# Tree attention on one core: ScalarE copies K out of PSUM, the transposes lead PE's iteration, GpSimd spreads a part of V

## The chip, the cores and the metric

One core of a Trainium2 chip. PE is its matrix engine; in this kernel PE's results stand in a memory called PSUM, and VectorE or ScalarE copies them to SBUF, the memory that the next steps read. The metric is the device time of one execution in microseconds, median of several; lower is better. The kernel before runs at 159.24 us (three runs, 158.61 to 160.22). Line numbers such as L263 in profile lines are those of each kernel's own file, so the same statement has another number in another kernel.

## The reference

Attention in which query i sees only itself and its ancestors in a binary tree over the sequence. Eight batches, twelve heads, 512 positions, 64 dimensions, float32.

```python
mask[i, i] = 1
parent = i
while parent > 0:
    parent = (parent - 1) // 2
    mask[i, parent] = 1
scores = np.einsum('bhqd,bhkd->bhqk', Q, K) * scale
scores = scores + (1 - mask) * (-1e9)
weights = np.exp(scores - np.max(scores, axis=-1, keepdims=True))
weights = weights / (np.sum(weights, axis=-1, keepdims=True) + 1e-10)
return np.einsum('bhqk,bhkd->bhqd', weights, V).astype(np.float32)
```

## The kernel before

The work is cut into 48 pairs of heads, six pairs a batch. Each pair goes through three steps: `transposes` (PE turns Q and K into PSUM, VectorE copies both to SBUF), `scores` (PE multiplies, ScalarE takes three exponentials), `values` (PE multiplies the weights with V, VectorE normalises, the result is stored). Besides, VectorE spreads V into a layout that the sparse products need ("V copies", two halves a batch, nine copies each). GpSimd issues the loads, which cast float32 to bf16 on the way.

```python
def load(b):                       # six stage buffers per tensor
    ...
    elif b < B - 1:
        plan = ((V, 0, H), (Q, 0, 6), (K, 0, 6), (Q, 6, H), (K, 6, H))
    else:
        plan = ((V, 0, H), (Q, 0, 6), (K, 0, 6), (Q, 6, 10), (K, 6, 10),
                (Q, 10, H), (K, 10, H))
    ...                            # one nc.gpsimd.dma_start per entry

def transposes(i):
    b, hp = pairs[i]
    if hp == 0:
        load(b)
    tp = psumT.tile([P, 2, 512], bf16)     # Q in [:, 0, :], K in [:, 1, :]
    ...                                    # 16 transposes on PE
    qk = work.tile([P, 2, 512], bf16)
    nc.vector.tensor_copy(out=qk[:, :, :], in_=tp[:, :, :])

# the loop; the order of PE, VectorE and ScalarE is the order of the program
for i in range(N):
    b, hp = pairs[i]
    if i + 1 < N:
        scores(i + 1)
    if i + 2 < N:
        transposes(i + 2)
    values(i)
    ...                                    # V copies of this or the next batch on VectorE
```

The softmax here doesn't subtract the row's maximum and nothing guards it: scores larger than these inputs give would overflow.

Of the kernel before, what the change touches and what calls it, by code (L numbers as in the profile page):

```python
# [123 lines left out]
def kernel(  # L124
# [7 lines left out]
    nc = tc.nc  # L132
    B, H, S, D = Q.shape
    P = nc.NUM_PARTITIONS
    assert (S, D) == (512, 64) and H % 2 == 0
    T = 4
    HP = H // 2
# [52 lines left out]
    def load(b):  # L190
        qs = stage.tile([P, H, T * D], bf16)
        ks = stage.tile([P, H, T * D], bf16)
        vs = stage.tile([P, H, T * D], bf16)
        if b == 0:
            plan = ((Q, 0, 2), (K, 0, 2), (V, 0, 6), (Q, 2, 6), (K, 2, 6),
                    (V, 6, H), (Q, 6, H), (K, 6, H))
# [5 lines that stand above are left out]
        for src, h0, h1 in plan:  # L202
            dst = qs if src is Q else ks if src is K else vs
            nc.gpsimd.dma_start(  # L204
                out=dst[:, h0:h1, :],
                in_=src[b, h0:h1].rearrange("h (p t) d -> p h (t d)", t=T),
            )
        loaded[b] = (qs, ks, vs)

    def spread(b, half):  # L210
        vs = loaded[b][2]
        v1, vx = v1s[b % NV], vxs[b % NV]
        n = H // 2
        h0, h1 = n * half, n * half + n
        v = vs[:, h0:h1, :].rearrange("p h (t d) -> p h t d", t=T)
        ops = [(vx[64:P, h0:h1, :, 0:D], v[64:P, :, :, :])]
        for par in range(2):
            slots = slice(0, 4, 3) if par else slice(1, 3)
            for a in range(2):
                ops.append((  # L220
                    vx[32 * a:32 * a + 32, h0:h1, slots, 0:D],
                    v[32:64, :, 2 * a + par, :].unsqueeze(2).to_broadcast(
                        [32, n, 2, D]
                    ),
                ))
        for r in range(T):
            ops.append((
                v1[32 * r:32 * r + 32, h0:h1, 0:D], v[0:32, :, ORD[r], :]
            ))
        return ops  # L230

    def copies(ops):
        for o, i in ops:
            nc.vector.tensor_copy(out=o, in_=i)  # L234
# [3 lines left out]

    def transposes(i):
        b, hp = pairs[i]  # L240
        if hp == 0:
            load(b)
        qs, ks, vs = loaded[b]
        tp = psumT.tile([P, 2, 512], bf16)

        for sel, src, order in ((0, qs, ident), (1, ks, permk)):
            for t in range(T):
                for hi in range(2):
                    o = tp[D * hi:D * hi + D, sel, :]
                    if sel == 0:  # L250
                        o = o[:, P * t:P * t + P]
                    else:
                        lo = 64 * ORD[t]
                        step = 256 + 64 * t - lo
                        o = o[:, lo:].rearrange(
                            "d (c x) -> d c x", x=64
                        )[:, 0:step // 64 + 1:step // 64, :]
                    nc.tensor.matmul(  # L258
                        out=o, lhsT=src[:, 2 * hp + hi, D * t:D * t + D],
                        rhs=order, start=True, stop=True, is_transpose=True,  # L260
                    )
        qk = work.tile([P, 2, 512], bf16)
        nc.vector.tensor_copy(out=qk[:, :, :], in_=tp[:, :, :])  # L263
        state[i] = qk

    def scores(i):
# [57 lines left out]
    def values(i):  # L324
        b, hp = pairs[i]
        v1, vx = v1s[b % NV], vxs[b % NV]
        et1, etx, ete = state.pop(i)
        o2 = psumO.tile([P, 2, 512], fp32)
        for hi in range(2):
            h = 2 * hp + hi  # L330
            for t in range(T):
                w = [(et1[:, hi, P * t:P * t + P], v1[:, h, 0:D + 1]),
                     (etx[:, hi, t, :], vx[:, h, t, 0:D + 1])]
                if t < 2:
                    w.append((ete[:, hi, 96 * t:96 * t + P],
                              vx[:, h, 1 - t, 0:D + 1]))
                for n, (e, v) in enumerate(w):
                    nc.tensor.matmul(  # L338
                        out=o2[:, hi, (D + 1) * t:(D + 1) * (t + 1)],
                        lhsT=e, rhs=v, start=n == 0, stop=n == len(w) - 1,  # L340
                    )
        o4 = o2[:, :, 0:T * (D + 1)].rearrange("p h (t x) -> p h t x", t=T)
        rec = opool.tile([P, 2, T, 1], fp32)
        nc.vector.reciprocal(out=rec[:, :, :, :], in_=o4[:, :, :, D:D + 1])  # L344
        of = opool.tile([P, 2, T * D], fp32)
        nc.vector.tensor_tensor(  # L346
            out=of[:, :, :].rearrange("p h (t d) -> p h t d", t=T),
            in0=o4[:, :, :, 0:D],
            in1=rec[:, :, :, :].to_broadcast([P, 2, T, D]),
            op=ALU.mult,  # L350
        )
        nc.sync.dma_start(
            out=out[b, 2 * hp:2 * hp + 2].rearrange(
                "h (p t) d -> p h (t d)", t=T
            ),
            in_=of[:, :, :],
        )

    N = len(pairs)
    E = mybir.EngineType  # L360
    with tc.manual_schedule(engines={E.PE, E.DVE, E.Activation}):
        transposes(0)
        scores(0)
        transposes(1)
        copies(spread(0, 0))
        todo = []
        for i in range(N):
            b, hp = pairs[i]
            if i + 1 < N:
                scores(i + 1)  # L370
            if i + 2 < N:
                transposes(i + 2)
            values(i)
            if hp == 0:
                todo = spread(b, 1)
            elif hp == HP - 2 and b + 1 < B:
                todo = spread(b + 1, 0)
            if hp in (0, 1, 2):
                lo, hi = ((0,) + (3, 6, 9))[hp:hp + 2]
                copies(todo[lo:hi])  # L380
            elif hp >= HP - 2 and b + 1 < B:
                copies(todo[0:4] if hp == HP - 2 else todo[4:9])


# [28 lines left out]
```

## Time and profile before

| | before |
|---|---|
| time, median | 159.24 us |
| profiled span | 158.6 us, granted PE clock 0.989 |
| busy PE / VectorE / ScalarE / GpSimd | 78 / 79 / 58 / 24 % |
| last load packet | 140.5 us |
| first to last normalising multiply | 19.91 to 154.47 us, 2.86 us a pair |

The prediction below shows the page's engine shares and slices. Read them as an average over a long middle, in which both VectorE and the DMA queues are full, and a last part after about 140 us in which only the engines work. Two more lines, from the page's chain of what ended last and from the view of waits, will be needed for comparison:

```profile
DMA 65%; DVE 19%; PE 6%; POOL 5%; issue 3%; POOLq 0%
```

```profile
ACT et L291 <- PE st L273: 60.0, 48, 6.7
```

The chain goes through loads for 65% of the span. ScalarE waited 60.0 us in total, 48 times (once a pair), and always for PE's scores.

### The profile page before, as it was taken

To read this page: it belongs to the slowest core of one execution; us is meant where nothing else is said; L and a number is where in the kernel's file an instruction comes from. 1 tells how busy PE (TensorE), PEld (TensorE's weight loads), DVE (VectorE), ACT (ScalarE), POOL (GpSimd) and SP (SyncE) were. 2 spreads that over 40 slices of the span, in tenths; PEclk is the share of its full clock that TensorE was granted. 3 is DMA by queue.
4 is the path that set the end of the run, shared out by engine and by line. 5 is a ranking of instruction groups with operands and counts; after the bars stand their busy time and mean duration, and the time that the engine had idled before them with its cause. 6 is when DMAs were issued, how large, how long until landed. Compare 5 with 4: busy or idle time off the path is not lost.

```text
span 158.6 us, 6339 instructions
## 1 busy us (share of the span) xinstructions
PE 123.9 (78%) x2784; PEld 82.8 (52%) x2784; DVE 125.0 (79%) x300; ACT 92.3 (58%) x145; POOL 38.2 (24%) x49
## 2 busy tenths in 40 slices
PE   0437698987889589968978789968998787968960
PEld 0213566654556357746655565745665654645640
DVE  4104889699988999799959999799969995799951
ACT  3041357665667458766674676855866668546840
POOL 7955412322242222420224222240321000000000
PEclk9999999999999999999999999999999999999995
DMA  5999999999999999999999999999999999622432
GB/s 117 145 174 197 201 195 221 235 231 227 227 232 227 238 222 223 245 228 229 225 228 239 220 223 238 225 243 221 223 244 221 231 233 237 179 81 72 133 107 94
DMA packets 50811, 32.23 MB, mean 203 GB/s; under 512 B 1504, under 2 KB 50656, under 8 KB 50784
## 3 DMA queue, kind: packets, MB, share of 16 engines
q0 software_dynamic: 37584, 18.88, 87.9%
q1 hardware_dynamic: 13200, 12.96, 28.8%
q8 instruction: 21, 0.34, 0.8%
q14 instruction: 6, 0.05, 0.1%
HBM read 38.13 MB, written 12.58 MB: 320 GB/s over the span
## 4 chain that ended last, share of the span: by engine, by line
DMA 65%; DVE 19%; PE 6%; POOL 5%; issue 3%; POOLq 0%
DMA ks<-in_K_dram 53%; DMA qs<-in_Q_dram 12%; DVE of L346 6%; DVE vx L234 6%; DVE qk L263 3%; PE o L338 3%; DVE v L234 3%; POOL vs L204 2%; DVE rec L344 2%; POOL qs L204 2%; POOL ks L204 1%; PE tp L258 1%; PE stx L273 1%; PE st L273 1%; POOLq L397 0%
## 5 line engine op out<-in xcount | busy, mean ns | idle before, releaser
L291 ACT ACTIVATE et<-st 128x1024 bf16<-128x1024 f32 x48 | 49.1, 1023 | 60.0 <-PE st L273 60.0
L263 DVE COPY qk<-tp 128x1024 bf16<-128x1024 bf16 x48 | 32.9, 685 | 20.0 <-PE tp L258 19.3
L338 PE MATMUL o<-v,et 128*128 128x65 bf16 x384 | 36.5, 195 | 10.2 <-DVE v L234 9.1
L273 PEld LDWEIGHTS <-qk 64*64 64x64 bf16 (+1 forms) x864 | 19.9, 108 | 36.9 <-issue 20.1
L312 ACT ACTIVATE etx<-stx 128x768 bf16<-128x768 f32 x48 | 38.7, 805 | 0.0
L338 PEld LDWEIGHTS <-et 128*128 128x128 bf16 x384 | 30.7, 98 | 14.5 <-DVE v L234 10.3
L338 PE MATMUL o<-vx,etx 128*128 128x65 bf16 x384 | 36.1, 194 | 0.0
L346 DVE TENSOR_TENSOR of<-o,rec 128x512 f32<-128x512 f32 x48 | 33.2, 692 | 1.7
L234 DVE COPY vx<-vs 32x768 bf16<-32x768 bf16 (+1 forms) x80 | 33.0, 412 | 1.6
L338 PEld LDWEIGHTS <-etx 128*128 128x128 bf16 x384 | 31.4, 98 | 1.2 <-issue 1.2
L338 PE MATMUL o<-vx,ete 128*128 128x65 bf16 x192 | 27.7, 195 | 0.0
L258 PE MATMUL tp<-ctile,qs 128*64 128x128 bf16 x384 | 20.9, 232 | 8.3 <-DMA qs<-in_Q_dram 8.3
L273 PE MATMUL st<-qk 64*128 64x512 bf16 x96 | 19.2, 396 | 8.5 <-DVE qk L263 8.1
L204 POOL DMA_DIRECT2D qs<-in_Q_dram x18 | 14.9, 826 | 43.8 <-DMA vs<-in_V_dram 29.9
L258 PE MATMUL tp<-ctile,ks 128*64 128x128 bf16 x384 | 19.6, 226 | 2.9 <-DMA ks<-in_K_dram 2.9
L204 POOL DMA_DIRECT2D ks<-in_K_dram x18 | 14.6, 809 | 26.4 <-DMA qs<-in_Q_dram 13.6
L273 PE MATMUL st<-ctile 64*128 64x512 bf16 x96 | 19.7, 400 | 0.3 <-issue 0.3
L273 PE MATMUL stx<-qk 64*64 64x64 bf16 (+2 forms) x768 | 19.9, 211 | 0.0
L338 PEld LDWEIGHTS <-ete 128*128 128x128 bf16 x192 | 18.4, 98 | 0.0
L234 DVE COPY v<-vs 32x384 bf16<-32x384 bf16 x64 | 17.6, 275 | 1.0
L258 PEld LDWEIGHTS <-qs 128*64 128x64 bf16 x384 | 12.8, 113 | 9.7 <-DMA qs<-in_Q_dram 8.4
L273 PE MATMUL stx<-ctile 64*128 64x448 bf16 x96 | 17.6, 363 | 0.0
(14 smaller groups left out, 59.2 us busy)
## 6 DMA issues: line engine op xcount, KB each, us to landing
out_dram<-of SPq DMA_DIRECT2D x48, 256.0 KB, 6.3
qs<-in_Q_dram POOLq DMA_DIRECT2D x14, 384.0 KB, 25.9
ks<-in_K_dram POOLq DMA_DIRECT2D x14, 384.0 KB, 26.1
vs<-in_V_dram POOLq DMA_DIRECT2D x7, 768.0 KB, 28.0
vs<-in_V_dram POOLq DMA_DIRECT2D x2, 384.0 KB, 8.9
qs<-in_Q_dram POOLq DMA_DIRECT2D x2, 256.0 KB, 17.1
ks<-in_K_dram POOLq DMA_DIRECT2D x2, 256.0 KB, 17.0
ctile<-tree_consts SPq DMA_DIRECT2D x1, 368.0 KB, 3.0
```

The lines of the kernel that those rows point to most:

```text
L204: nc.gpsimd.dma_start(out=dst[:, h0:h1, :], in_=src[b, h0:h1].rearrange("h (p t) d -> p h (t d)", t=T),)
L234: nc.vector.tensor_copy(out=o, in_=i)
L258: nc.tensor.matmul(out=o, lhsT=src[:, 2 * hp + hi, D * t:D * t + D], rhs=order, start=True, stop=True, is_transpose=True,)
L263: nc.vector.tensor_copy(out=qk[:, :, :], in_=tp[:, :, :])
L273: nc.tensor.matmul(out=dst, lhsT=lhsT, rhs=rhs, start=first, stop=True, skip_group_check=not first,)
L291: nc.scalar.activation(out=et1[:, :, :], in_=st1[:, :, :], func=AF.Exp, scale=scale)
L312: nc.scalar.activation(out=etx[:, :, :, 32:P], in_=stx[:, :, 0:384].rearrange("p h (c q) -> p h c q", c=T), func=AF.Exp, scale=scale,)
L338: nc.tensor.matmul(out=o2[:, hi, (D + 1) * t:(D + 1) * (t + 1)], lhsT=e, rhs=v, start=n == 0, stop=n == len(w) - 1,)
L344: nc.vector.reciprocal(out=rec[:, :, :, :], in_=o4[:, :, :, D:D + 1])
L346: nc.vector.tensor_tensor(out=of[:, :, :].rearrange("p h (t d) -> p h t d", t=T), in0=o4[:, :, :, 0:D], in1=rec[:, :, :, :].to_broadcast([ ...
```

## The change

The intent is to take work off VectorE. ScalarE copies the K half of each transposed tile, GpSimd takes three of the nine V copies of each half, and PE does the transposes of pair i+2 ahead of the scores of pair i+1, so that the copies have longer. As GpSimd's order is now fixed by the program, loads are issued one batch ahead by hand.

```diff
-        ops = [(vx[64:P, h0:h1, :, 0:D], v[64:P, :, :, :])]
+        ops = []
 ...
-        return ops
+        ops.insert(0, (vx[64:P, h0:h1, :, 0:D], v[64:P, :, :, :]))
+        for o, i in ops[0:3]:
+            nc.gpsimd.tensor_copy(out=o, in_=i)
+        return ops[3:]
 ...
-        if hp == 0:
-            load(b)
+        if hp == 0 and b + 1 < B:
+            load(b + 1)
 ...
-        nc.vector.tensor_copy(out=qk[:, :, :], in_=tp[:, :, :])
+        nc.vector.tensor_copy(out=qk[:, 0, :], in_=tp[:, 0, :])
+        nc.scalar.copy(out=qk[:, 1, :], in_=tp[:, 1, :])
 ...
-    with tc.manual_schedule(engines={E.PE, E.DVE, E.Activation}):
+    with tc.manual_schedule(engines={E.PE, E.DVE, E.Activation, E.Pool}):
+        load(0)
 ...
+            if i + 2 < N:
+                transposes(i + 2)
             if i + 1 < N:
                 scores(i + 1)
-            if i + 2 < N:
-                transposes(i + 2)
             values(i)
 ...                                  # the V copies left to VectorE shared out anew: 2, 2, 2 and 3, 3
```

More of the change, by code (lines that the diff above doesn't have):

```diff
@@ L378 @@
             if hp in (0, 1, 2):
-                lo, hi = ((0,) + (3, 6, 9))[hp:hp + 2]
+                lo, hi = (0, 2, 4, 6)[hp:hp + 2]
                 copies(todo[lo:hi])
             elif hp >= HP - 2 and b + 1 < B:
-                copies(todo[0:4] if hp == HP - 2 else todo[4:9])
+                copies(todo[0:3] if hp == HP - 2 else todo[3:6])
 _INS = ['Q', 'K', 'V']
```

## The prediction

> **What bounds the kernel now.** I read the whole-run page first (engine shares, the 40 slices, the queue lines), then GpSimd's own timeline, the timeline around one stall, and the groups. The page:
>
> ```profile
> PE 123.9 (78%) x2784; PEld 82.8 (52%) x2784; DVE 125.0 (79%) x300; ACT 92.3 (58%) x145; POOL 38.2 (24%) x49
> ...
> DVE  4104889699988999799959999799969995799951
> ACT  3041357665667458766674676855866668546840
> ...
> DMA  5999999999999999999999999999999999622432
> ...
> q0 software_dynamic: 37584, 18.88, 87.9%
> q1 hardware_dynamic: 13200, 12.96, 28.8%
> ```
>
> Two things look full: VectorE (nine tenths in most slices) and the 16 DMA engines (nine tenths from slice 2 to slice 34, that is to about 139 us; then six tenths and less). VectorE invites the reading "the kernel is VectorE bound, so take work off it", which is the intent of the change. GpSimd's timeline says which of the two leads. GpSimd keeps eight loads in flight, so each issue is released by the landing of the load eight places before it. The V issues of a batch are released by the landing of the first K chunk of the batch two before; the last batch is split more finely, and there a Q issue is released by that of batch 6:
>
> ```profile
> 46.54 1.01 POOL L204 DMA_DIRECT2D vs<-in_V_dram  x1 [1.68 <-DMA ks<-in_K_dram]
> ...
> 63.90 1.01 POOL L204 DMA_DIRECT2D vs<-in_V_dram  x1 [2.37 <-DMA ks<-in_K_dram]
> ...
> 83.05 1.01 POOL L204 DMA_DIRECT2D vs<-in_V_dram  x1 [2.17 <-DMA ks<-in_K_dram]
> ...
> 100.43 1.01 POOL L204 DMA_DIRECT2D vs<-in_V_dram  x1 [2.54 <-DMA ks<-in_K_dram]
> ...
> 117.06 0.70 POOL L204 DMA_DIRECT2D qs<-in_Q_dram  x1 [1.92 <-DMA ks<-in_K_dram]
> ```
>
> So the first K chunk of batches 2 to 6 landed at about 46.5, 63.9, 82.6 (the chain of waits has it ending there), 100.4 and 117.0, and the timeline below shows that of batch 7 at 135.0: (135.0 - 46.5)/5 = 17.7 us a batch. VectorE's multiply that normalises a pair ("of") starts at 55.83 for the first pair of batch 2 and 72.82 for batch 3, where no load is waited for: 17.0 us a batch. The two are within 4%, and the loads are the slower. The packets agree: 37584/8 + 13200/8 = 6348 packets a batch, and in the middle of the run each engine finishes one every 43.8 ns (2920 packets per 8 us on 16 engines, counted in the trace), so 6348 x 43.8/16 = 17.4 us.
>
> The stall at the last batch, then VectorE in the rows of the groups:
>
> ```profile
> 134.70 0.28 ACT L317 ACTIVATE ete<-stx 128x128 bf16<-128x128 f32 x1
> ...
> 135.04 0.41 PE L258 MATMUL tp<-ctile,ks 128*64 128x128 bf16 x8 [1.11 <-DMA ks<-in_K_dram]
> 135.50 0.69 DVE L263 COPY qk<-tp 128x1024 bf16<-128x1024 bf16 x1 [2.08 <-PE tp L258]
> ```
>
> The reader is to see that at 135.0 all engines had run dry and PE started again on a landing. Eight pairs (40 to 47) are still to be normalised; their multiplies start at 136.45 ... 154.47, and the span ends at 158.6. The end is therefore: landing of the last batch's first K chunk (135.0) plus a tail of 23.6 us. Only the tail can be shortened by faster engines; 135.0 is set by the queues.
>
> **What the Trainium skill says.** (1) "SBUF — State Buffer", Who interferes with whom: VectorE in a two-port mode and GpSimd hold a shared port pair exclusively, the other waits. The trace agrees: the 384-element V copy has a median of 251 ns, and this one, started inside a GpSimd issue, took 0.62 us and ended with it:
>
> ```profile
> 24.50 0.82 POOL L204 DMA_DIRECT2D qs<-in_Q_dram  x1 [4.22 <-DMA vs<-in_V_dram]
> ```
> ```profile
> 24.75 0.62 DVE L234 COPY v<-vs 32x384 bf16<-32x384 bf16 x1
> ```
>
> (2) "GPSIMD Engine Reference", 4.1 Engine selection: an operation with one input runs at roughly line rate; its section 3.1 gives 1.03 cycles an element for short bodies and 2.6 for two inputs. No row of this trace has a GpSimd copy. (3) "ScalarE: Activation LUTs", What ACT_TABLE_LOAD costs: 186 ns + 0.833 ns an element, neighbours overlapping by 93 ns. Agrees: 1024, 768 and 128 elements took 1023, 805 and 284 ns, and the busy total 92.3/48 = 1.92 us a pair is less than their sum, 2.11, by two overlaps of 0.09. (4) "VectorE: DVE Perf Modes", Why PSUM operands drop a tier: at most two elements a cycle from PSUM; the 1024-element copy at 685 ns (533 + about 150) fits.
>
> **The change part by part.** Rows used:
>
> ```profile
> L291 ACT ACTIVATE et<-st 128x1024 bf16<-128x1024 f32 x48 | 49.1, 1023 | 60.0 <-PE st L273 60.0
> L263 DVE COPY qk<-tp 128x1024 bf16<-128x1024 bf16 x48 | 32.9, 685 | 20.0 <-PE tp L258 19.3
> ...
> L346 DVE TENSOR_TENSOR of<-o,rec 128x512 f32<-128x512 f32 x48 | 33.2, 692 | 1.7
> ...
> L234 DVE COPY vx<-vs 32x768 bf16<-32x768 bf16 x64 | 23.7, 371 | 1.1
> L234 DVE COPY v<-vs 32x384 bf16<-32x384 bf16 x64 | 17.6, 275 | 1.0
> ```
>
> VectorE a pair before: 0.685 + 0.692 + 0.20 (reciprocal) + V copies 50.5/48 = 1.05, sum 2.63, plus gaps of some 0.2: the 2.83 us of 17.0/6. After: the Q half of the copy is 512 elements, about 0.42 (267 + 150 ns); a batch keeps 4 + 8 of its 18 V copies, 4 x 0.371 + 8 x 0.275 = 3.7 us or 0.61 a pair. Sum 0.42 + 0.69 + 0.20 + 0.61 = 1.92, with gaps 2.1. It frees 0.7 us a pair.
>
> ScalarE gains a 512-element copy, about 0.60 us by the slope between its rows ((1023 - 284)/896 = 0.825 ns an element), 0.51 where it overlaps: 1.92 + 0.51 to 0.60 = 2.4 to 2.5 us a pair. It becomes the fullest engine beside PE, whose tightest pair before took 2.35 us (63.78 to 66.13). I expect 2.5 us a pair where nothing else waits.
>
> PE's order: transposes first gives the copies of Q and K a whole iteration before the scores need them, which takes away PE's waits for qk (8.1 us at matmuls, mostly hidden now). It costs something at a stall: a late K chunk now holds back the scores of the pair before, which before were already done.
>
> GpSimd gains per batch 2 copies of 1536 and 4 of 768 elements. At one element a cycle of 1.2 GHz and 0.2 us each (an estimate from the GPSIMD page): 2 x 1.5 + 4 x 0.84 = 6.4 us, beside five issues of about 0.85. The built order shows five loads of the next batch, then the six copies, with no load issued between. So issuing pauses 6.4 us a batch. With eight loads in flight and one landing every 3.5 us, five or more stay queued: the DMA engines stay full. The first copies wait until the fifth issue of batch 1, at about 14.3; the first half is spread at about 17.5, and the first value products before began at 18.4. No loss.
>
> So until the last K chunk nothing moves: 17.4 to 17.7 us a batch from the queues, engines able to do 15. T stays 135.0. The tail from T: K transposes 0.45; scores and first exponential of pair 41 to T+2.0; its remaining exponentials to T+2.95; five more pairs at 2.5 bring pair 46 to T+15.5; pair 47 without a copy in front, +1.9 = T+17.4; value products 0.75, reciprocal 0.25, so the last multiply starts at T+18.4, against 154.47 - 135.04 = T+19.4 before. The rest (multiply, store, 4.1 us) is unchanged. Gain 1.0 us: 159.24 - 1.0 = 158.2.
>
> **The rivals.** (A) VectorE leads, not the queues: then 17.0 us a batch becomes 15, eight batches save 16 us, about 143. For it: VectorE's slices at 9. Against it: the landings 17.7 us apart with full DMA slices, and PE waiting for K at five places; 7.5 batches of queue work cannot shrink. I give it 5%, even in a small form (155). (B) GpSimd's copies are slow. At 2.6 cycles an element the six take 13.5 us; with issues 17.7, just the pace of the queues; above that GpSimd sets the pace and every 1 us costs 8. (C) The lock: VectorE's two-port copies (350 ns for 768 elements is four a cycle) wait for whole GpSimd copies. Those of a batch start about when its first Q chunk lands, and VectorE's own copies of that batch start some 5 us later, so short GpSimd copies collide with two or three, 1 to 2 us a batch inside a slack of 5; slow ones could collide with seven and cost more than the slack. B and C together would give 162 to 175. (D) ScalarE at 2.7 rather than 2.5 us a pair: still under 2.9, the queues' pace, but the tail is then 1.4 us longer: 159.5.
>
> **Range and chances.** Centre 158.2. Low 156.0: the tail at PE's 2.35 a pair saves 1.9, and T may come 1 us earlier. High 161.5: D, with a late V spread in batch 6, whose GpSimd copies stand behind the finer-split last loads (issued till 120.7) and could hold PE 1 to 3 us if slow. Faster by over 2% (below 156.05) 0.10; within 0.76; slower (above 162.4) 0.14.
>
> **What would show it.** Right: DMA slices still 9 to about slice 34, first K chunks landing 17 to 18 us apart and the last at 134 to 136; VectorE's busy time near 95 us and ScalarE's near 118; a GpSimd copy of 1536 elements at 1.3 to 1.7 us; PE idle mostly put down to loads; the last eight multiplies 2.5 us apart. Wrong: DMA slices below 9 in the middle with K chunks further apart (B), V copies on VectorE far above 371 ns (C), or K chunks landing earlier (A: the queues were held back by something I did not see).

## The result, and the profile after

The changed kernel takes 182.97 us (four runs, 182.8 to 187.37) against 159.05 for before with one more run: a ratio of 1.149, 95% interval 1.141 to 1.157. Ratios here are the mean time of one kernel's fast runs over that of the other's fast runs of the same rounds, so they are not quite the ratio of the medians quoted. Executions over 1.5% slower than the fastest of the same kernel are left out of the means. The profiled execution of the changed kernel was its slowest (187.37 us).

The page of the changed kernel, engine shares, slices and chain:

```profile
PE 132.5 (72%) x2784; PEld 93.1 (50%) x2784; DVE 112.3 (61%) x252; ACT 114.6 (62%) x193; POOL 87.6 (47%) x97
...
DVE  3019778487465947495684775585844685457511
ACT  2321456874855568847568776729578867796750
...
DMA  6999999999999999999999999996131322133122
...
DMA 25%; PE 21%; DVE 18%; ACT 18%; issue 10%; POOL 5%; ACTq 0%; POOLq 0%
```

No engine is full any more, and the DMA engines are no longer full after slice 27 (about 125 us; the last load packet ended at 129.4, before at 140.5). The chain no longer hangs on one thing: DMA 25% where it was 65%, and PE, VectorE and ScalarE share the rest. That is the picture of engines that wait for one another in turn. From the first to the last normalising multiply the kernel now takes 22.02 to 180.78 us, 3.38 us a pair instead of 2.86: 47 x 0.515 = 24.2 us, with the 2.1 us later start all of the 26.3 us between the two spans.

The loads did not end early because they were faster. The queues share the engines between loads and stores: when the last load packet ended, 8143 of 13056 store packets had been moved, before 11135. With the pairs slower, fewer stores competed.

The waits of the changed kernel (total us, times, longest):

```profile
ACT qk L267 <- DVE qk L266: 62.2, 32, 6.5
...
DVE rec L348 <- PE o L342: 52.8, 40, 2.9
PE st L277 <- ACT et L295: 26.4, 20, 3.3
```

ScalarE's idle time is as long as before (62.2 against 60.0), but it stands elsewhere: not before the exponential for PE, but before the new K copy, for VectorE's Q copy. VectorE in turn waits for PE's value products and PE for ScalarE's exponentials. The timeline of the changed kernel, at a point where no loads and no GpSimd copies are left, shows the loop once (start us, duration, engine, instruction; in brackets the idle time before it and what ended it):

```profile
148.42 0.30 ACT L321 ACTIVATE ete<-stx 128x128 bf16<-128x128 f32 x1
...
148.63 0.38 PE L277 MATMUL st<-qk 64*128 64x512 bf16 x2
...
148.91 0.71 DVE L237 COPY vx<-vs 32x768 bf16<-32x768 bf16 x2
...
149.65 0.42 DVE L266 COPY qk<-tp 128x512 bf16<-128x512 bf16 x1
150.11 0.59 ACT L267 COPY qk<-tp 128x512 bf16<-128x512 bf16 x1 [1.39 <-DVE qk L266]
...
150.59 1.03 ACT L295 ACTIVATE et<-st 128x1024 bf16<-128x1024 f32 x1
...
151.68 0.39 PE L277 MATMUL st<-ctile 64*128 64x512 bf16 x2 [0.86 <-ACT et L295]
```

ScalarE was free at 148.72. The scores for its next exponential were done at 149.01. But in its order the K copy comes first, and that waits until VectorE, which first spread V and then copied Q, is done at 150.07. The exponential starts at 150.59, 1.6 us later than its data allowed, and 1.39 us of that is the copy's wait. PE then waits 0.86 us, because the scores have one PSUM buffer. In the next pair PE is late, VectorE has caught up and nothing waits; so long and short pairs alternate, 3.86, 2.34, 3.71, 2.36 us between multiplies from 144.33 on, 3.04 on average.

Why does one copy wait for the other? They write different halves of `qk` and read different halves of `tp`. The built program has a wait for the Q copy of the same pair at each of the 48 K copies, and it puts each `tp` whole (2 KiB a partition) into one bank of PSUM. The Trainium skill, "PSUM — Partial Sum Buffer", section "PSUM bank collisions raise a hardware error", says that two engines must not access one bank and 32-partition quadrant at once, reads by ScalarE and VectorE and disjoint columns included, and that the compiler back end's scheduler adds a dependency for it. I had not looked that page up. The experiments test whether this wait is the cause.

The durations themselves came out as expected. Groups of the changed kernel (busy us, mean ns):

```profile
L237 DVE COPY v<-vs 32x384 bf16<-32x384 bf16 x64 | 32.0, 501 | 1.0
L267 ACT COPY qk<-tp 128x512 bf16<-128x512 bf16 x48 | 28.4, 592 | 62.3 <-DVE qk L266 62.2
L232 POOL COPY vx<-vs 32x768 bf16<-32x768 bf16 x32 | 26.3, 821 | 1.9
L232 POOL COPY vx<-vs 64x1536 bf16<-64x1536 bf16 x16 | 23.4, 1463 | 2.7 <-DMA vs<-in_V_dram 1.8 <-PE o L342 0.2
...
L266 DVE COPY qk<-tp 128x512 bf16<-128x512 bf16 x48 | 20.2, 420 | 11.8 <-PE tp L261 10.5
L237 DVE COPY vx<-vs 32x768 bf16<-32x768 bf16 x32 | 17.5, 545 | 0.7
```

The K copy, the Q copy and GpSimd's two copies are what the prediction gave them. VectorE's own V copies are not: 501 ns for 275, 545 for 371. That is 64 x 0.226 + 32 x 0.174 = 20 us of waiting inside the instructions. It goes with GpSimd's copies (262 ns in e6_nopool, which has none), and I take it for the port lock of the prediction's first point.

### The profile page after: what moved, and what is told of

It reads as the page before. It is cut to its first block, busy times and chain, and to the rows that moved or that the text cites. A ratio compares the mean times of both kernels' runs of the same rounds, so it can differ in the third digit from the quotient of the medians.

```text
span 184.9 us, 6437 instructions
## 1 busy us (share of the span) xinstructions
PE 132.5 (72%) x2784; PEld 93.1 (50%) x2784; DVE 112.3 (61%) x252; ACT 114.6 (62%) x193; POOL 87.6 (47%) x97
## 4 chain that ended last, share of the span: by engine, by line
DMA 25%; PE 21%; DVE 18%; ACT 18%; issue 10%; POOL 5%; ACTq 0%; POOLq 0%
DMA qs<-in_Q_dram 11%; ACT et L295 10%; DMA vs<-in_V_dram 9%; PE o L342 9%; PE stx L277 8%; ACT etx L316 6%; DVE v L237 5%; DVE vx L237 5%; DMA ks<-in_K_dram 4%; DVE of L350 3%; POOL vx L232 3%; DVE qk L266 3%; PE st L277 2%; DVE rec L348 2%; ACT ete L321 2%
## 5 line engine op out<-in xcount | busy, mean ns | idle before, releaser
L267 ACT COPY qk<-tp 128x512 bf16<-128x512 bf16 x48 | 28.4, 592 | 62.3 <-DVE qk L266 62.2
L232 POOL COPY vx<-vs 32x768 bf16<-32x768 bf16 (+1 forms) x48 | 49.7, 1035 | 4.5 <-DMA vs<-in_V_dram 1.8
L342 PE MATMUL o<-v,et 128*128 128x65 bf16 x384 | 39.7, 202 | 7.1 <-DVE v L237 6.0
L348 DVE RECIPROCAL rec<-o 128x8 f32<-128x8 f32 x48 | 9.9, 206 | 53.0 <-PE o L342 52.8
L277 PEld LDWEIGHTS <-ctile 64*128 64x128 bf16 x192 | 15.1, 96 | 51.5 <-issue 41.5
L342 PE MATMUL o<-vx,etx 128*128 128x65 bf16 x384 | 39.5, 201 | 0.0
L342 PEld LDWEIGHTS <-etx 128*128 128x128 bf16 x384 | 33.6, 102 | 4.4 <-issue 4.4
L342 PEld LDWEIGHTS <-et 128*128 128x128 bf16 x384 | 32.9, 103 | 4.3 <-DVE v L237 1.7
L237 DVE COPY v<-vs 32x384 bf16<-32x384 bf16 x64 | 32.0, 501 | 1.0
L266 DVE COPY qk<-tp 128x512 bf16<-128x512 bf16 x48 | 20.2, 420 | 11.8 <-PE tp L261 10.5
## 6 DMA issues: line engine op xcount, KB each, us to landing
ks<-in_K_dram POOLq DMA_DIRECT2D x14, 384.0 KB, 24.2
```

The costliest lines, as they stand in the source:

```text
L232: nc.gpsimd.tensor_copy(out=o, in_=i)
L237: nc.vector.tensor_copy(out=o, in_=i)
L266: nc.vector.tensor_copy(out=qk[:, 0, :], in_=tp[:, 0, :])
L267: nc.scalar.copy(out=qk[:, 1, :], in_=tp[:, 1, :])
L277: nc.tensor.matmul(out=dst, lhsT=lhsT, rhs=rhs, start=first, stop=True, skip_group_check=not first,)
L342: nc.tensor.matmul(out=o2[:, hi, (D + 1) * t:(D + 1) * (t + 1)], lhsT=e, rhs=v, start=n == 0, stop=n == len(w) - 1,)
```

## The experiments

Theory 1: the loss is the chain "exponentials stand behind the K copy, the K copy waits for the Q copy, the Q copy stands behind the previous pair's normalisation and V copies". Theory 2: the port lock makes the loss. Theory 3: PE's new order makes it. All kernels gave correct results. Each ran on one chip with runs of before beside it (medians 159.78, 160.17 and 160.10 us); the ratio is to those.

**e1_swap.** The two copies exchanged in program order, nothing else:

```diff
-        nc.vector.tensor_copy(out=qk[:, 0, :], in_=tp[:, 0, :])
         nc.scalar.copy(out=qk[:, 1, :], in_=tp[:, 1, :])
+        nc.vector.tensor_copy(out=qk[:, 0, :], in_=tp[:, 0, :])
```

> The changed kernel with only the two copies exchanged in program order: ScalarE's K copy first, VectorE's Q copy second, so that now VectorE is made to wait for ScalarE and ScalarE waits for no VectorE instruction of the same pair. Theory 1 (the exponentials stand behind the K copy, which waits for VectorE's Q copy of the same tile, which stands behind the previous pair's normalisation and V copies): 158 to 164 us, ScalarE's idle time before its K copy no longer put down to VectorE. Theory 2 (the port lock between GpSimd's and VectorE's V copies): unchanged, 178 to 185. Theory 3 (transposes leading PE's order): unchanged, 178 to 185.

Measured: 163.7 us median; three of four runs (163.37 to 164.15) are slow against the one of 160.71, but either figure is some 20 us below the changed kernel. Its waits (the profile is of a slow run) have, at the head:

```profile
ACT qk L266 <- PE tp L261: 29.4, 21, 5.7
```

and the timeline near its end:

```profile
148.14 0.69 DVE L350 TENSOR_TENSOR of<-o,rec 128x512 f32<-128x512 f32 x1
...
148.49 0.60 ACT L266 COPY qk<-tp 128x512 bf16<-128x512 bf16 x1
...
149.06 1.02 ACT L295 ACTIVATE et<-st 128x1024 bf16<-128x1024 f32 x1
...
149.28 0.42 DVE L267 COPY qk<-tp 128x512 bf16<-128x512 bf16 x1
...
150.48 0.69 DVE L350 TENSOR_TENSOR of<-o,rec 128x512 f32<-128x512 f32 x1
```

ScalarE's copy follows its last exponential at once and the next exponential follows the copy; VectorE comes after, when it has time (its wait for ScalarE's copy is 12.9 us over the run, 9 times). Multiplies are 2.34 us apart. The same copies, the same GpSimd work and the same PE order as in the changed kernel, and the loss is gone with the direction of one wait. Theories 2 and 3 expected no effect.

**e2_twotiles.** Q and K in two PSUM tiles (one bank each, single-buffered, so two banks in all, as before) and two SBUF tiles:

```diff
-        tp = psumT.tile([P, 2, 512], bf16)          # psumT with bufs=2
+        tpq = psumT.tile([P, 512], bf16)            # psumT with bufs=1
+        tpk = psumT.tile([P, 512], bf16)
 ...
-        nc.vector.tensor_copy(out=qk[:, 0, :], in_=tp[:, 0, :])
-        nc.scalar.copy(out=qk[:, 1, :], in_=tp[:, 1, :])
+        nc.vector.tensor_copy(out=qt_[:, :], in_=tpq[:, :])
+        nc.scalar.copy(out=kt_[:, :], in_=tpk[:, :])
```

> The changed kernel with the Q and K transposes in two PSUM tiles (each single, same number of banks) and two SBUF tiles, so that neither copy waits for the other. Theory 1: 157 to 164 us, as for the exchange. Theory 2 and theory 3: 178 to 185. If single buffering costs something itself, PE shows waits for the copies before its transposes, and it may be 2 to 5 us above the exchange.

Measured: 160.72 us (158.81 to 161.12), ratio 1.005 (0.998 to 1.012): same as before. In the built program the wait on VectorE is gone from the K copies. Two variants were built but not run: with only the SBUF tile split, all 48 K copies wait for the Q copy of their pair; with only the PSUM tile split (a bank each), none does. So the wait belongs to the shared PSUM tile, which fits the skill's page, and it is the cause of the loss. The page speaks of the compiler's back end; here the wait is already in the program that the back end is given. Whether that was decided by bank or by tile is not shown. Both theory 1 forecasts held.

**e3_oldorder.** PE's old order (scores, transposes, values) in the changed kernel; this also puts the K copy behind the exponentials in ScalarE's order.

```diff
-            if i + 2 < N:
-                transposes(i + 2)
             if i + 1 < N:
                 scores(i + 1)
+            if i + 2 < N:
+                transposes(i + 2)
```

> The changed kernel with PE's old order in an iteration (scores, then transposes, then values), which also puts ScalarE's K copy behind the exponentials. Theory 1: the exponentials no longer stand behind the K copy, but the next scores need it: about 2.8 to 3.0 us a pair, 158 to 166 us. Theory 2: 178 to 185. Theory 3: back to about 159.

Measured: 168.87 us, ratio 1.055 (1.047 to 1.063). The multiplies of the last two batches are 2.91 to 3.00 us apart up to pair 45, as expected, but the total missed the range by 3 us. It is far below 178, so the lock alone does not make the loss; it is well above 159, so the old order does not cure everything: the scores now wait for the K copy (PE's score matmuls 20.9 us, 43 times).

**e4_dvecopy.** VectorE copies Q and K in one instruction again; transposes still lead, GpSimd still spreads.

> The changed kernel with VectorE copying Q and K in one instruction again; transposes still lead, GpSimd still spreads its part. Theory 1: 157 to 162 us, because no ScalarE instruction waits for VectorE's copies any more. Theory 2: still 172 to 185, VectorE's 384-element V copies still about 500 ns instead of 275. Theory 3: still 172 to 185.

Measured: 161.34 us, ratio 1.009 (1.003 to 1.015), V copies of 384 elements still 505 ns:

```profile
L237 DVE COPY v<-vs 32x384 bf16<-32x384 bf16 x64 | 32.3, 505 | 1.0
```

The lock is all there and the transposes lead, and the loss is gone.

**e6_nopool.** The changed kernel with all nine V copies back on VectorE, GpSimd only issuing:

```diff
-        for o, i in ops[0:3]:
-            nc.gpsimd.tensor_copy(out=o, in_=i)
-        return ops[3:]
+        return ops                      # shared out over the iterations as before
```

> The changed kernel with all V copies back on VectorE, nothing else undone (one tile, K copy waits for Q copy, transposes lead). Theory 1: the chain stays and VectorE has more of its own V work in it (1.05 us a pair against 0.61 plus the lock), 172 to 186 us. Theory 2 (the lock makes the loss): 157 to 162 us.

Measured: 184.58 us, ratio 1.154 (1.144 to 1.163). No GpSimd copies, no lock, and the full loss. Its profile shows the same wait, with V copies as short as before:

```profile
ACT qk L265 <- DVE qk L264: 58.9, 36, 5.3
```

```profile
L235 DVE COPY v<-vs 32x384 bf16<-32x384 bf16 x64 | 16.7, 262 | 1.0
```

**e7_kcopy_alone, e11_order_alone, e12_pool_alone.** One part of the change each. All three, and every row of the table below but the first, keep the hand-issued loads of the change.

> Before with the K copy on ScalarE as the one part of the change (old order, V all on VectorE). Theory 1: K copy behind the exponentials and behind the Q copy, the next scores wait for it: 2.9 to 3.0 us a pair as in the run with the old order, 164 to 170 us. If the loss needs the transposes in front, 157 to 161.

> Before with transposes leading PE's iteration as the one part of the change. Theory 1: no ScalarE copy, no chain; VectorE is the fullest engine as before: 158 to 161 us. Theory 3: clearly slower, above 170.

> Before with GpSimd spreading its part of V as the one part. Theory 1: the lock stretches VectorE's V copies (275 to about 500 ns), which eats most of what it is spared: 158 to 162 us. Theory 2: clearly slower, above 170.

Measured: 162.99 us (ratio 1.019, 1.011 to 1.026, unclear; between the two ranges given), 161.58 (two of four runs slow, the fast ones 159.53 and 160.85; 1.002, 0.990 to 1.013, same) and 161.43 (1.011, 1.003 to 1.020, unclear; V copies of 384 elements at 469 ns). With before and the changed kernel, all eight combinations have been run:

| K copy on ScalarE | transposes lead | GpSimd spreads | median us | ratio |
|---|---|---|---|---|
| no | no | no | 159 to 160 | 1 |
| yes | no | no | 162.99 | 1.019 |
| no | yes | no | 161.58 | 1.002 |
| no | no | yes | 161.43 | 1.011 |
| no | yes | yes | 161.34 | 1.009 |
| yes | no | yes | 168.87 | 1.055 |
| yes | yes | no | 184.58 | 1.154 |
| yes | yes | yes | 182.97 | 1.149 |

The first two parts cost about 2% or less alone and 15% together. The pair makes the loss because both are needed: the copy creates the wait, and the order of the program puts the wait ahead of the exponentials. The table also shows a smaller pair: the K copy with GpSimd's spreading costs 5.5%, more than their 1.9% and 1.1%; no run says why.

**e5_twotiles_nopool, e8_fine_chunks, e9_early_spread, e10_early_fine.** With the chain gone the question was whether the freed engines could beat before. e2_twotiles ran at about 2.4 us a pair in its last batch, but had a hole around pairs 35 to 38. VectorE's and GpSimd's timelines there, each in its own fence:

```profile
122.47 2.96 DVE L237 COPY v<-vs 32x384 bf16<-32x384 bf16 x3
```

```profile
119.69 6.49 POOL L232 COPY vx<-vs 64x1536 bf16<-64x1536 bf16 x6
```

Three V copies took 2.96 us inside GpSimd's six; without GpSimd three take 0.78 (in e5). e5 takes GpSimd's copies away from e2. e8 also loads the last batch's Q and K two heads at a time. e9 keeps GpSimd's copies and runs those of each batch ahead of the issue of the next batch's loads. e10 is e9 with the fine chunks.

```diff
+            plan = ((V, 0, H),) + tuple(          # e8 and e10, last batch only
+                (src, h, h + 2) for h in range(0, H, 2) for src in (Q, K)
+            )
+            if hp == HP - 3 and b + 1 < B:        # e9 and e10: GpSimd's part of V early
+                spread(b + 1, 0, True)
+                spread(b + 1, 1, True)
```

> The two-tile kernel with all V copies back on VectorE and GpSimd only issuing loads. If the hole of about 8 us over pairs 35 to 38 in the runs that no longer wait for the Q copy (multiplies 5.3 and 3.3 us apart there, 2.34 to 2.6 elsewhere) comes from GpSimd's late copies of batch 6 and the port lock, it closes: first K chunk of batch 7 at about 135, tail of about 21 us, 156 to 159 us. If the hole has another cause, it stays and the time is 160 to 162.

> The two-tile kernel without GpSimd copies, and the last batch's Q and K loaded two heads at a time. If the end is the landing of the last batch's first K chunk plus a tail, the first chunk is now a third as large and lands about 4 us earlier, each pair follows its own chunk at the queues' pace (about 2.9 us), and what is left behind the last landing (about 140.5) is two to three pairs: 151 to 155 us. If the end is set by the engines' total work, no gain over the kernel with the usual chunks.

> The two-tile kernel with GpSimd's copies of each batch moved ahead of the issue of the next batch's loads, so that they run right after that batch's V landed, some 4 us earlier against VectorE's own V copies (8 us earlier for batch 6). If the hole over pairs 35 to 38 comes from the port lock between the two engines' copies, the V copies on VectorE shorten from 447 ns towards 300, the hole closes and the time is 155 to 159 us. If the hole has another cause: 160 to 162, V copies shortened or not. The queues must stay full; a DMA slice under 9 before slice 33 would be a cost of the move.

> The same with the last batch's Q and K loaded two heads at a time. If engines at 2.35 to 2.6 us a pair follow the landings to the end: 151 to 156 us. If the engines are still behind the landings at batch 7, no gain over the run before it.

Measured: e5 161.61 us (1.011), e8 159.70 (0.999), e9 161.18 (1.005), e10 161.32 (1.010), every one outside what I expected of the better case. By the time alone e5 and e9 fall into the range given for "another cause" than the lock; what follows is read from their traces. In e5 pairs 35 to 38 take 12.1 us instead of e2's 15.3, which speaks for the lock, but with all V copies VectorE's long iterations come back: the last six pairs up to pair 45 are 3.47, 2.85, 3.26, 2.61, 2.59 and 2.62 us apart, 17.4 in all against before's 18.0. In e8 PE's wait of 0.94 us for the last batch's first K chunk in e5 is gone, but pair 40 was normalised at 137.26 us, the same as in e5 (137.31), so the engines were not waiting for that landing any more. In e9 pairs 35 to 38 are 2.36 to 2.63 us apart, so the hole went; VectorE's view of it:

```profile
112.43 1.68 DVE L238 COPY v<-vs 32x384 bf16<-32x384 bf16 x2
...
115.44 1.95 DVE L238 COPY v<-vs 32x384 bf16<-32x384 bf16 x2
...
125.48 0.79 DVE L238 COPY v<-vs 32x384 bf16<-32x384 bf16 x3
```

The slow copies are now at 112 to 117 us, which is where GpSimd's copies of that batch now stand (112.54 to 119.03); at 125 three copies take 0.79. The hole moved with GpSimd's copies (pairs 33 and 34 are now 3.79 and 3.69 us apart), which is what the lock would do. But the V copies are longer on average (545 ns, in e2 447), and the last load packet ended at 142.3 us, in e2 at 137.2: GpSimd now waited 44.5 us for V to land with no loads issued meanwhile. None of the runs beats before; whether a kernel can have 2.34 us a pair without the lock, and full queues, is left open.

## Why the prediction was wrong, point by point

1. **What bounds before.** Nothing contradicted it, but for one misread figure: slice 34 ends at 134.8 us, not at about 139. e2, e4, e8 and e9 run their engines at 2.34 to 2.6 us in part of the pairs and end within 1% of before. "T stays 135.0", though, took the queues' share as fixed. It holds only while the engines keep up: with slow engines the loads ended 11 us sooner, as fewer stores competed, and set nothing.
2. **Durations.** The K copy came to 592 ns (0.60 predicted), the Q copy 420 (0.42), GpSimd's copies 1463 and 821 (1.5 and 0.84; the 0.2 us a copy in that estimate is not on the page named for it, and 0.18 was measured). VectorE's busy time was 112.3 us (near 95 predicted); the difference, 17, is of the size of the lock's 20 us. "No loss" at the first spread was wrong: VectorE's six copies there took 6.6 us inside GpSimd's six, and the first value products began at 20.5 instead of 18.4 us.
3. **The step that failed** is "ScalarE gains a 512-element copy, about 0.60 us ... 2.4 to 2.5 us a pair", together with "transposes first gives the copies of Q and K a whole iteration before the scores need them". The first counts the copy as a duration. The second asks when the copy's result is needed. Neither asks what the copy must wait for and what stands behind it in ScalarE's order. It waited for the Q copy 62.2 us in 32 waits, and the exponentials stood behind it. "Engines able to do 15" us a batch was 6 x 3.04 = 18.2 us even where neither loads nor GpSimd took part, and 3.38 x 6 = 20.3 over the run. e1_swap and e2_twotiles take away only that wait and end at 160 to 164 us; e6_nopool takes the lock away and keeps the loss.
4. **Rival C**, the lock, was put at 1 to 2 us a batch: 20 us over 8 batches is 2.5. It costs 1% alone (e12_pool_alone), I suppose because it lies in VectorE's slack, and it shows as the hole at batch 6, for which the late V spread had been named as a risk. It made no part of the large loss that a run could show: without it the time is 184.58.
5. **Rivals A, B and D.** GpSimd's copies were not slow (at B's 2.6 cycles, with the 0.2 us a copy that the estimate before it has, the six would take 14.5 us, not 13.5), and ScalarE's busy time was 114.6 us, near the 118 given. No rival named a wait between the two copies.
6. **What would show it wrong** listed landings and V copies, not an idle ScalarE. The decisive line was the first of the waits.

A smaller effect was not separated: the granted PE clock of the two slow combinations was 0.913 to 0.958, that of before's fast runs beside the experiments 0.973 to 0.997. Value matmuls took 202 ns instead of 195, at most 3.6% of PE's busy time, too little for 15%, and it came with a PE that keeps stopping.

## What to carry to other kernels

When a copy is moved to another engine, write down three things, not one: how long it takes, what it waits for, and what stands behind it in that engine's order. In this program two engines that read halves of one PSUM tile were serialised, 48 times of 48; give each its own tile (here also its own bank), or let the engine with work queued behind the copy go first. Two parts that cost about 2% or less each can cost 15% together, so test pairs as well as single parts before blaming the part that looks most suspicious.

## What the Trainium skill lacked or had wrong

- "PSUM — Partial Sum Buffer", section on bank collisions: what it says of an added dependency between ScalarE and VectorE fits, and would have pointed at the failed step; I had not looked it up. (No run here had a collision.) What it lacks is the price: here 62.2 us of ScalarE's waits in a span of 184.9 us, and 160.72 instead of 182.97 us with a bank for each reader.
- "SBUF — State Buffer", Who interferes with whom: agrees. It gives no size for many short copies: 384-element VectorE copies rose from 275 to 501 ns on average, and three of them took 2.96 us beside GpSimd's copies instead of 0.78.
- "GPSIMD Engine Reference", section 4.1: "roughly line-rate" for one input is borne out, but no figure is given for a bf16 copy, nor for the fixed part. Here 821 ns for 768 and 1463 for 1536 elements: 0.836 ns an element and 0.18 us fixed.
- "ScalarE: Activation LUTs": its 186 ns + 0.833 ns an element gives 613 ns for the 512-element copy, if the copy is taken for an ACTIVATE; 592 measured.
